# Turning the residual sum x2 (three of four column groups) and the input p by VectorE's 32x32 blocks out of DRAM instead of by TensorE

## The chip, the cores and the metric

The kernel runs on one core of a Trainium2 chip. Its time is the device time of one execution in microseconds (us); lower is better. The time before is the median of three runs, 1085.27 us (1084.38 to 1087.19).

## The reference

One decoder layer on 512 positions and 2048 channels, all in float32. Cut to what matters here:

```
h = rms_norm(x, norm_g);  z = h @ w_in                  # 2048 -> 6272 columns
y_rwkv = ...             # 16 heads x 64, delta-rule recurrence over 512 positions, gate
y_pool = ...             # 4 groups x 256, trailing means, small linear map, gate
y_mix  = concat(y_rwkv, y_pool)
x2  = x + y_mix @ w_out
gate = sigmoid(x2 @ w_pg + b_pg)
x3  = x2 + gate * (p @ w_ple)
out = rms_norm(x3, final_g)
```

A matrix product on TensorE contracts over the partition axis. `x2 @ w_pg` therefore needs x2 with its channels on the partitions, while the sum `x + y_mix @ w_out` comes out with positions on the partitions. The same holds for `p @ w_ple`. So x2 and p must be turned (transposed) before they can be multiplied.

## The kernel before, in words

Every large product is made of three matmuls in fp32r (`mm3`, L155 to L158): each operand is split into a rounded part `hi` and a rest `lo`, and hi·hi, hi·lo and lo·hi are added up in PSUM. A weight tile is loaded by a DMA that SyncE's queue issues (`raw`, L129), ScalarE makes `whi` by a cast (L132), VectorE makes `wlo` by a subtraction (L133). `raw`, `whi` and `wlo` have four buffers each, so the DMA of a tile waits until the subtraction of the tile four places earlier is done, and a cast waits until TensorE has used up the tile four places earlier.

The program has these stages:

1. RMSNorm of x, and x turned into `hhi`/`hlo`.
2. The head stage: eight pairs of heads, one after another (`recur`, `gather`, `prepare`, `scores`, `invert`). A pair's recurrence is a chain TensorE, VectorE, TensorE, ScalarE over eight chunks. TensorE never waits for it idly: between its steps `pump(n)` puts in n matmuls of a long stream (`stream`), which holds the z projections of later pairs, the pool group (`pool_unit`) and, in the last pair, the embedding product (`embed_unit`). In this stage TensorE keeps program order. The job `"p"` of the stream turns p: eight 128x128 transposes on TensorE into the PSUM tile `ppt`, each half then split into `phi` and `plo`. p itself comes by two DMAs that ScalarE's queue issues into `pn` (L927), which takes the buffer that `ar` of the last pair but one leaves.
3. The output projection: four column groups `ec` of 512 columns. Each has 16 steps (one weight tile of `w_out` per step, in the order of `order`), and each step has 12 matmuls: four position tiles times three. The sums stand in four of five PSUM accumulators that go round. At a group's end VectorE adds x to the four accumulators (L1026, tile `x2_{ec}_{tt}`; the trace calls it `x`), ScalarE's queue writes each sum to DRAM (`x2d`, L1027), and `turn` (L1029) turns it: 16 transposes on TensorE into PSUM (`px`, L1033), then four casts (L137) and four subtractions (L138) into `x2hi` and `x2lo`. For the first three groups `turn` runs right behind the group. For the last it runs as `aside`, inside the first group of the next stage.
4. The gate: the product with `w_pg` in four column groups, 16 steps each. The sum x2 is read back from `x2d` (`fetch`, L1133), and gate, embedding and final norm follow per position tile.

Instructions outside the head stage are placed by a scheduler with priorities; each engine then runs its own list in order, and so does each DMA queue.

Of the kernel before, what the change touches and what calls it, by code (L numbers as in the profile page):

```python
# [9 lines left out]
F32 = mybir.dt.float32  # L10
# [3 lines left out]
ALU = mybir.AluOpType  # L14

P = 128
T = 512
D = 2048
KT = D // P
NT = T // P  # L20
# [5 lines left out]
DPLE = 256  # L26
# [8 lines left out]
def trunk_kernel(ctx: ExitStack, tc: tile.TileContext, x, p, norm_g, w_in, mu, w0, w_up, a0, a_up,  # L35
                 k_k, k_a, r_k, ln_w, ln_b, w_pool, pool_scale, w_out, w_ple, w_pg, b_pg, final_g, out):
    nc = tc.nc
    PSUM = bass.MemoryType.PSUM
    x, p, w_in, w_out, w_ple, w_pg = x[0], p[0, 0], w_in[0], w_out[0], w_ple[0], w_pg[0]
    out = out[0]  # L40

    cst = ctx.enter_context(tc.tile_pool(name="cst", bufs=1))
    dram = ctx.enter_context(tc.tile_pool(name="dram", bufs=2, space=bass.MemoryType.DRAM))
# [4 lines left out]
    psM = s2.enter_context(tc.tile_pool(name="psM", bufs=3, space=PSUM))  # L48
# [24 lines left out]
    ident = cst.tile([P, P], F32, name="ident")  # L73
# [20 lines left out]
    for h in range(2):  # L94
        rows = slice(64 * h, 64 * h + 64)
# [30 lines left out]

    def wsplit(src, kt, n, nm):
        raw = wp.tile([P, kt, n], F32, name=f"raw_{nm}", tag="raw")
        nc.sync.dma_start(out=raw, in_=src)  # L129
        hi = wp.tile([P, kt, n], F32R, name=f"whi_{nm}", tag="whi")  # L130
        lo = wp.tile([P, kt, n], F32R, name=f"wlo_{nm}", tag="wlo")
        nc.scalar.copy(hi, raw)  # L132
        nc.vector.tensor_tensor(lo, raw, hi.bitcast(F32), ALU.subtract)  # L133
        return hi, lo

    def split(hi, lo, src):
        c_ = nc.scalar.copy(hi, src)  # L137
        nc.vector.tensor_tensor(lo, src, hi.bitcast(F32), ALU.subtract)  # L138
        return c_
# [20 lines left out]
    def tr(*a):  # L160
        i = nc.tensor.transpose(*a)
        return tc.keep_in_program_order(i) if pin[0] else i

    def mm3(ps, wh, wl, xh, xl, first, last):
        mm(ps, wh, xh, start=first, stop=False)
        mm(ps, wh, xl, start=False, stop=False)
        return mm(ps, wl, xh, start=False, stop=last)
# [26 lines left out]
    EC = 512  # L194
# [12 lines left out]
    for kind, nm, j in jobs:  # L207
# [7 lines left out]
        else:  # L215
            g, i = j // 4, j % 2
# [7 lines left out]
    order = [8, 9, 10, 11, 12, 13, 0, 1, 2, 3, 4, 5, 6, 7, 14, 15]  # L224
# [47 lines left out]
    pt = psM.tile([P, T], F32, name="pt_prm", tag="m")  # L272
# [188 lines left out]
    def stream():  # L461
        for kind, nm, j in jobs:
            if kind == "b":
                yield from pool_unit(j)
                continue
            if kind == "e":
                yield from embed_unit(j)
                continue
            if kind == "p":
                for k in range(2):  # L470
                    pt = psM.tile([P, T], F32, name=f"ppt{k}", tag="m")
                    for tt in range(NT):
                        tr(pt[:, tt * P:(tt + 1) * P], pn[0][:, tt, k * P:(k + 1) * P], ident)
                    a_ = rw.tile([P, T], F32R, name=f"phi{k}", tag=("sk", "sr")[k], bufs=2)
                    b_ = rw.tile([P, T], F32R, name=f"plo{k}", tag=("sv", "sg")[k], bufs=2)
                    split(a_, b_, pt)
                    phl.append((a_, b_))
                yield 3
                continue
            ps = psA.tile([P, T], F32, name=f"z{nm}{j}", tag="acc")  # L480
            yield from zcols(ps, f"{nm}{j}")
            t_ = rw.tile([P, T], F32, name=f"s{nm}{j}", tag=f"s{nm}", bufs=2)
            if nm == "g":
                silu2(ps, t_)
            else:
                shifted(ps, t_, {"r": 0, "k": 8, "v": 16}[nm] + j)
            zt[nm, j] = t_
# [429 lines left out]
    for j in range(NJ):  # L917
        def between():
            pump(H3 if j + 1 < NJ else HC[2])
            if j + 1 < NJ:  # L920
                scores(j + 1)
                pump_to(H2)

        if j + 1 == NJ:
            pn.append(rw.tile([P, NT, DPLE], F32, name="pn", tag="ar", bufs=2))
            for h in range(2):
                nc.scalar.dma_start(out=pn[0][:, 2 * h:2 * h + 2, :],  # L927
                                    in_=p[256 * h:256 * h + 256, :].rearrange("(t p) q -> p t q", p=P))
        if j + 1 < NJ:
            prepare(j + 1)  # L930
        elif gates:
            gates.pop()()
        recur(j, invert(j + 1) if j + 1 < NJ else iter(()), between)
        if j + 1 < NJ:
            gather(j + 1)
# [21 lines left out]

    x2hi = hp.tile([P, KT, T], F32R, name="x2hi", tag="ahi")
    x2lo = hp.tile([P, KT, T], F32R, name="x2lo", tag="alo")
    x2d = dram.tile([T, D], F32, name="x2d", bufs=1)  # L960

    KEEP, LATE = 8, 4
    TP = 40
# [4 lines left out]
        pool, tag = (psB, "accb") if nacc[0] % 5 in (1, 2, 3) else (psA, "acc")  # L968
        return pool.tile([P, EC], F32, name=nm, tag=tag)

    def proj(w, hi_, lo_, ec, nm, ks=range(KT), tts=range(NT), keep=None, aside=None):
        acc = {tt: acc_tile(f"acc_{nm}{ec}_{tt}") for tt in tts}
        for i, k in enumerate(ks):
            src = w[k * P:(k + 1) * P, ec * EC:(ec + 1) * EC].unsqueeze(1)
            if nm == "o" and ec == 0 and i + AHEAD < KT:
                load_y(ks[i + AHEAD])
            if (f"{nm}{ec}_{k}", 0) in ready:
                wh, wl = ready.pop((f"{nm}{ec}_{k}", 0))
            elif nm == "o" and ec == 0 and i < 4:
                wh, wl = chunk(f"{nm}{ec}_{k}", 0)  # L980
            elif keep is None or LATE <= i < KT - KEEP:
                wh, wl = wsplit(src, 1, EC, f"{nm}{ec}_{k}")
            else:
                raw = wp.tile([P, 1, EC], F32, name=f"raw_{nm}{ec}_{k}", tag="raw")
                nc.sync.dma_start(out=raw, in_=src)
                if i < 2:
                    if i == 0:
                        two = [pp.tile([P, 2, EC], F32R, name=f"{g}k", tag=g, bufs=1) for g in ("dh", "dl")]
                    wh, wl = (g[:, i:i + 1, :] for g in two)
                else:  # L990
                    own = i < KT - 4
                    wh, wl = ((kp_ if own else wp).tile([P, 1, EC], F32R, name=f"{g}k{k}",
                                                        tag=f"{g}k{k}" if own else g) for g in ("whi", "wlo"))
                split(wh, wl, raw)
                keep[k] = (wh, wl)
                if i >= LATE:
                    continue
            for tt in tts if keep is None or i >= LATE else tts[:-1]:
                ts_ = slice(tt * P, (tt + 1) * P)
                first = i == (LATE if keep is not None and tt == NT - 1 else 0)  # L1000
                e_ = mm3(acc[tt], hi_[:, k, ts_], lo_[:, k, ts_], wh[:, 0, :], wl[:, 0, :], first, i == KT - 1)
            if aside is not None and i == 2:
                with tc.issue_after(e_.ins):
                    hi = aside()
                with tc.issue_after(hi.ins):
                    recall(0, lp)
        return acc

    ples = {}

    def recall(ec, pool):
        ples[ec] = []
        for tt in range(NT):
            t_ = pool.tile([P, EC], F32, name=f"pler{ec}_{tt}", tag="ple", bufs=4)
            nc.scalar.dma_start(out=t_, in_=pled[tt * P:(tt + 1) * P, ec * EC:(ec + 1) * EC])
            ples[ec].append(t_)

    for ec in range(D // EC):
        es = slice(ec * EC, (ec + 1) * EC)
        acc = proj(w_out, yhi, ylo, ec, "o", order)  # L1020
        x2 = []
        for tt in range(NT):
            rows = slice(tt * P, (tt + 1) * P)
            t_ = pp.tile([P, EC], F32, name=f"x2_{ec}_{tt}", tag=("u", "sw")[tt // 2])
            nc.scalar.dma_start(out=t_, in_=x[rows, es])
            nc.vector.tensor_tensor(t_, acc[tt], t_, ALU.add)  # L1026
            nc.scalar.dma_start(out=x2d[rows, es], in_=t_)  # L1027
            x2.append(t_)
        def turn(ec=ec, x2=x2):  # L1029
            for i in range(EC // P):  # L1030
                pt = psM.tile([P, T], F32, name=f"px2_{ec}_{i}", tag="m")
                for tt in range(NT):
                    nc.tensor.transpose(pt[:, tt * P:(tt + 1) * P], x2[tt][:, i * P:(i + 1) * P], ident)  # L1033
                hi = split(x2hi[:, 4 * ec + i, :], x2lo[:, 4 * ec + i, :], pt)
            return hi


        if ec < D // EC - 1:
            turn()

    sy.close()

# [1 line left out]
    with tc.tile_pool(name="fp", bufs=2) as fp, tc.tile_pool(name="kp_", bufs=1) as kp_:  # L1044
# [86 lines left out]

        def fetch(ec, tt):
            x2_ = fp.tile([P, EC], F32, name=f"x2r{ec}_{tt}", tag="x2r", bufs=4)  # L1133
            nc.scalar.dma_start(out=x2_, in_=x2d[tt * P:(tt + 1) * P, ec * EC:(ec + 1) * EC])
            pre[tt] = (x2_, ple[tt])

        for ec in range(LAST):
# [74 lines left out]
```

## Time and profile before

| | |
|---|---|
| median of 3 runs | 1085.27 us (1084.38 to 1087.19) |
| the profiled execution | 1082.7 us, of which the span of its instructions is 1081.0 us |
| TensorE (PE) busy | 1056.6 us, 98% of the span |
| VectorE (DVE) busy | 714.0 us, 66% |
| ScalarE (ACT) busy | 441.5 us, 41% |
| DMA | 146.94 MB, mean 136 GB/s |

How to read the views. PE is TensorE's matmuls, PEld its weight loads, which run beside them; DVE is VectorE, ACT is ScalarE, SPq and ACTq are the DMA queues that SyncE and ScalarE feed. Times count from the start of the span. A matmul's own duration is modelled and overlaps the next one's, so what a matmul costs TensorE is read from the distance between starts, not from its mean duration. The chain of waits is followed back from the last instruction: each row is a stretch in which that work alone held up the end.

### The profile page before, as it was taken

How to read it: one execution, taken by the hardware profiler on the slowest of the kernel's cores; microseconds unless marked ns; L12 is line 12 of the kernel's file. 1: busy time of each engine (PE TensorE's matmuls, PEld its weight loads, DVE VectorE, ACT ScalarE, POOL GpSimd, SP SyncE). 2: the span in 40 equal slices, each digit the busy share in tenths (PEclk: the TensorE clock that was granted, in tenths of full speed). 3: DMA queues.
4: the chain of work that ended last, by engine and by line, in shares of the span. 5: the costliest groups of instructions: out<-in, count | busy, mean ns of one | idle time of the engine just before them, and what ended most of it. 6: DMA issues, size and time to landing. Idle time of an engine off the chain costs nothing.

```text
span 1081.0 us, 17106 instructions
## 1 busy us (share of the span) xinstructions
PE 1056.6 (98%) x5996; PEld 872.1 (81%) x5996; DVE 714.0 (66%) x1851; ACT 441.5 (41%) x901; POOL 75.0 (7%) x180
## 2 busy tenths in 40 slices
PE   5999999999999999999999999999999999999996
PEld 4888878888888887878788788888888888888885
DVE  6676978888779789787887857563432424445356
ACT  7633435335335354353352344553222222333337
POOL 2100010110110100200101201000000000000000
PEclk9999999999999999999999999999999999999999
DMA  7434443342634533434435343774434428355434
GB/s 236 117 115 111 139 116 88 116 120 74 168 88 114 144 89 105 120 89 112 106 91 158 100 129 111 239 243 141 171 121 143 166 98 271 122 182 161 169 98 156
DMA packets 212916, 146.94 MB, mean 136 GB/s; under 512 B 68085, under 2 KB 173150, under 8 KB 212830
## 3 DMA queue, kind: packets, MB, share of 16 engines
q1 hardware_dynamic: 192126, 112.28, 35.9%
q10 hardware_dynamic: 20704, 33.56, 9.4%
q8 instruction: 47, 0.77, 0.3%
q14 instruction: 39, 0.32, 0.1%
HBM read 122.21 MB, written 23.07 MB: 134 GB/s over the span
## 4 chain that ended last, share of the span: by engine, by line
PE 91%; DVE 4%; DMA 3%; ACT 2%; issue 1%; ACTq 0%; SPq 0%; DVEq 0%
PE acc_o L157 16%; PE acc_g L157 16%; PE zb L157 14%; PE zv L157 8%; PE zg L157 8%; PE zr L157 8%; PE zk L157 7%; PE py L157 2%; PE pu L157 2%; PE pple L157 2%; PE pm L157 1%; DMA n<-nd 1%; PE pp L157 1%; PE ps L157 1%; DMA xt<-in_x_dram 1%; PE pmv L157 1%
## 5 line engine op out<-in xcount | busy, mean ns | idle before, releaser
L133 DVE TENSOR_TENSOR wlo_g<-raw_g,whi_g 128x512 fp32r<-128x512 f32 x84 | 57.0, 685 | 74.4 <-ACT whi_g L132 72.3
L157 PE MATMUL zb<-hhi,whi_b 128*128 128x512 f32 x256 | 106.0, 414 | 0.0
L133 DVE TENSOR_TENSOR wlo_o<-raw_o,whi_o 128x512 fp32r<-128x512 f32 x64 | 43.9, 690 | 90.9 <-ACT whi_o L132 90.8
L157 PE MATMUL zb<-hhi,wlo_b 128*128 128x512 f32 x256 | 100.4, 392 | 0.0
L157 PE MATMUL acc_o<-whi_o,ylo 128*128 128x512 f32 x256 | 100.2, 391 | 0.0
L157 PE MATMUL acc_o<-whi_o,yhi 128*128 128x512 f32 x256 | 99.9, 390 | 0.0
L157 PE MATMUL zb<-hlo,whi_b 128*128 128x512 f32 x256 | 99.8, 390 | 0.0
L157 PE MATMUL acc_o<-wlo_o,yhi 128*128 128x512 f32 x256 | 99.7, 389 | 0.0
L132 ACT CAST whi_g<-raw_g 128x512 fp32r<-128x512 f32 x84 | 52.0, 621 | 105.3 <-PE acc_g L157 58.9
L157 PE MATMUL acc_g<-whi_g,x2hi 128*128 128x512 f32 x208 | 81.2, 391 | 0.0
L832 POOL TENSOR_SCALAR s0p<-sbd,pw 64x64 f32<-64x64 f32 x96 | 58.0, 604 | 332.0 <-DVE sbd L825 243.5
L157 PE MATMUL acc_g<-wlo_g,x2hi 128*128 128x512 f32 x208 | 80.9, 389 | 0.0
L157 PE MATMUL acc_g<-whi_g,x2lo 128*128 128x512 f32 x208 | 80.6, 389 | 0.0
L132 ACT CAST whi_o<-raw_o 128x512 fp32r<-128x512 f32 x64 | 39.9, 623 | 96.3 <-PE acc_o L157 96.3
L132 ACT CAST whi_b<-raw_b 128x512 fp32r<-128x512 f32 x64 | 39.7, 621 | 86.7 <-PE zb L157 29.2
L133 DVE TENSOR_TENSOR wlo_b<-raw_b,whi_b 128x512 fp32r<-128x512 f32 x64 | 43.6, 683 | 27.3 <-ACT whi_b L132 27.1
L157 PEld LDWEIGHTS zb<-hhi,wlo_b 128*128 128x128 f32 x256 | 48.0, 188 | 10.9
L678 DVE TENSOR_TENSOR xw<-xw,tm 128x60 f32<-128x60 f32 (+24 forms) x248 | 52.1, 210 | 7.0
L157 PEld LDWEIGHTS acc_o<-wlo_o,yhi 128*128 128x128 f32 x256 | 48.1, 188 | 9.9
L157 PEld LDWEIGHTS acc_o<-whi_o,ylo 128*128 128x128 f32 x256 | 48.1, 188 | 9.8
L157 PEld LDWEIGHTS acc_o<-whi_o,yhi 128*128 128x128 f32 x256 | 48.1, 188 | 9.7
L157 PEld LDWEIGHTS zb<-hhi,whi_b 128*128 128x128 f32 x256 | 48.2, 188 | 8.3
(283 smaller groups left out, 2529.6 us busy)
## 6 DMA issues: line engine op xcount, KB each, us to landing
raw_b<-in_w_in_dram SPq DMA_DIRECT2D x64, 256.0 KB
raw_o<-in_w_out_dram SPq DMA_DIRECT2D x64, 256.0 KB
raw_g<-in_w_pg_dram SPq DMA_DIRECT2D x64, 256.0 KB
raw_k<-in_w_in_dram SPq DMA_DIRECT2D x32, 256.0 KB
raw_r<-in_w_in_dram SPq DMA_DIRECT2D x32, 256.0 KB
raw_v<-in_w_in_dram SPq DMA_DIRECT2D x32, 256.0 KB
raw_g<-in_w_in_dram SPq DMA_DIRECT2D x32, 256.0 KB
bkd<-bk SPq DMA_DIRECT2D x8, 512.0 KB
```

The lines of the kernel that those rows point to most:

```text
L132: nc.scalar.copy(hi, raw)
L133: nc.vector.tensor_tensor(lo, raw, hi.bitcast(F32), ALU.subtract)
L157: i = nc.tensor.matmul(*a, **k)
L678: nc.vector.tensor_tensor(xw[:, 0:n_, s + 1:32], xw[:, 0:n_, s + 1:32], tm[:, 0:n_, 0:w_], ALU.add)
L832: nc.gpsimd.tensor_scalar(s0p[hc, :], nxt[hc, hc], pcn[hc], None, ALU.mult)
```

## The change

- **x2, groups 0 to 2.** `x2d` is laid out anew, as (column group, 128-column chunk, position, 128 columns). The 16 transposes on TensorE of each of these groups are gone. Instead the blocks are read back from `x2d` by 16 DMAs on SyncE's queue into `x2g`: a DMA brings 32 columns of a chunk, for all 512 positions, as 512 pieces of 128 bytes, so that block (b, q) lies where VectorE's transpose of 32x32 blocks turns it into place. VectorE then turns a chunk with one instruction of 128x512 (`STREAM_TRANSPOSE`, into `x2t`), and the split into `x2hi`/`x2lo` follows as before, out of SBUF instead of PSUM. This hangs in the next group's steps (`side`): reads from step 5 on, three DMAs a step, and turns at steps 8, 9, 11 and 12, each placed behind that step's weight DMA, cast and subtraction.
- **x2, group 3** is turned by TensorE as before. Its place (`aside`) moves by one step: it now stands before the third step's products, not behind them.
- **p** is read in the same blocked way by eight DMAs of 64 KB on SyncE's queue (two of 256 KB on ScalarE's before), and turned by two VectorE instructions instead of eight transposes on TensorE.
- **x2d** is now written, and read by `fetch`, in pieces of 512 bytes instead of 2048.

```diff
-                for k in range(2):
-                    pt = psM.tile([P, T], F32, name=f"ppt{k}", tag="m")
-                    for tt in range(NT):
-                        tr(pt[:, tt * P:(tt + 1) * P], pn[0][:, tt, k * P:(k + 1) * P], ident)
+                    pt = rw.tile([P, T], F32, name=f"ppt{k}", tag=("kk", "kp")[k])
+                    nc.vector.transpose(pt.rearrange("p (b k) -> p b k", k=32), pn[0][:, k])
...
-            for h in range(2):
-                nc.scalar.dma_start(out=pn[0][:, 2 * h:2 * h + 2, :],
-                                    in_=p[256 * h:256 * h + 256, :].rearrange("(t p) q -> p t q", p=P))
+            for q in range(4):
+                for c in range(2):
+                    nc.sync.dma_start(out=pn[0][32 * q:32 * q + 32, c],
+                                      in_=p[:, c * P + 32 * q:c * P + 32 * q + 32].rearrange("(b k) i -> k b i", k=32))
...
-    x2d = dram.tile([T, D], F32, name="x2d", bufs=1)
+    x2d = dram.tile([D // EC, EC // P, T, P], F32, name="x2d", bufs=1)
...
-            for tt in tts if keep is None or i >= LATE else tts[:-1]:
-                ...
             if aside is not None and i == 2:
...
+            if side is not None:
+                side(i)
+            for tt in tts if keep is None or i >= LATE else tts[:-1]:
+                ...
...
+    RD0, RDN, TURNS = 5, 3, (8, 9, 11, 12)
...
-        acc = proj(w_out, yhi, ylo, ec, "o", order)
+        acc = proj(w_out, yhi, ylo, ec, "o", order, side=side)
...
-            nc.scalar.dma_start(out=x2d[rows, es], in_=t_)
+            nc.scalar.dma_start(out=x2d[ec, :, rows, :].rearrange("c t e -> t c e"),
+                                in_=t_.rearrange("p (c e) -> p c e", e=P))
...
+        def turner(blocks, turned, ec=ec):
+            parts = [(c, q) for c in range(EC // P) for q in range(4)]
+
+            def side(i):
+                with tc.issue_after(wmade[0].ins), tc.issue_after(wmade[1].ins), tc.issue_after(wmade[2].ins):
+                    if i >= RD0:
+                        for c, q in parts[:RDN]:
+                            nc.sync.dma_start(out=blocks[32 * q:32 * q + 32, c],
+                                              in_=x2d[ec, c].rearrange("(b k) (q i) -> q k b i", k=32, i=32)[q])
+                        del parts[:RDN]
+                    if i in TURNS:
+                        c = TURNS.index(i)
+                        t_ = turned(c)
+                        nc.vector.transpose(t_.rearrange("p (b k) -> p b k", k=32), blocks[:, c])
+                        split(x2hi[:, 4 * ec + c, :], x2lo[:, 4 * ec + c, :], t_)
...
-            turn()
+            side = turner(ymp.tile([P, EC // P, T // 32, 32], F32, name=f"x2g{ec}", tag="x2g"),
+                          lambda i: ymp.tile([P, T], F32, name="x2t", tag="x2t"))
```

What the scheduler made of it is seen in two places. The first is SyncE's list in the second group of the output projection, in the changed kernel; `raw_o1_k` is the weight tile of row block k, and since the order of the steps is 8, 9, ..., 13, 0, 1, 2, ..., the tile `raw_o1_2` belongs to step 8.

```order
L129 DMA raw_o1_0_8542<-in_w_out_dram 128x512
L129 DMA raw_o1_1_8563<-in_w_out_dram 128x512
L1045 DMA x2g0_8426<-x2d_8101 32x16x32 x9
L129 DMA raw_o1_2_8584<-in_w_out_dram 128x512
L1045 DMA x2g0_8426<-x2d_8101 32x16x32 x3
L129 DMA raw_o1_3_8609<-in_w_out_dram 128x512
L1045 DMA x2g0_8426<-x2d_8101 32x16x32 x3
L129 DMA raw_o1_4_8634<-in_w_out_dram 128x512
L1045 DMA x2g0_8426<-x2d_8101 32x16x32
L129 DMA raw_o1_5_8653<-in_w_out_dram 128x512
```

Before, the weight tiles stand alone there. Now nine of the block reads stand between the tiles of steps 7 and 8, three between 8 and 9, three between 9 and 10, and one between 10 and 11.

The second place is VectorE's list at `gather` of the last pair. `y17` is the turned diagonal block of that pair's inverse (it is read from `x17`, which a DMA brings), for which TensorE's next product of the chain (`pq`) waits; `wlo_b12_k` is a weight tile of the stream, `ysb6` the scaling of the pair before. First the kernel before:

```order
L732 STREAM_TRANSPOSE y17_7360<-x17_7214 32x256
L133 TENSOR_TENSOR wlo_b12_0_4333<-raw_b12_0_4330,whi_b12_0_4332 128x512
L732 STREAM_TRANSPOSE y17_7360<-x17_7214 32x256
L873 TENSOR_SCALAR ysb6_6780<-ysb6_6780,mvr6_7284,rs86_7301 128x64 x6
L133 TENSOR_TENSOR wlo_b12_1_4355<-raw_b12_1_4352,whi_b12_1_4354 128x512
```

And the changed kernel:

```order
L133 TENSOR_TENSOR wlo_b12_0_4333<-raw_b12_0_4330,whi_b12_0_4332 128x512
L734 STREAM_TRANSPOSE y17_7360<-x17_7214 32x256
L133 TENSOR_TENSOR wlo_b12_1_4355<-raw_b12_1_4352,whi_b12_1_4354 128x512
L734 STREAM_TRANSPOSE y17_7360<-x17_7214 32x256
L875 TENSOR_SCALAR ysb6_6780<-ysb6_6780,mvr6_7284,rs86_7301 128x64 x8
```

Each half of `y17` now stands one weight subtraction later. On SyncE's list the reads of p now stand among the DMAs that carry the inverse. On TensorE's list nothing moves but this: the 8 + 48 transposes are gone, the transposes of group 3 stand 12 matmuls earlier, and in steps 8 to 11 of the groups the matmuls that need `whi` alone are drawn ahead of those that need `wlo`.

More of the change, by code (lines that the diff above doesn't have):

```diff
@@ L128, in wsplit @@
         raw = wp.tile([P, kt, n], F32, name=f"raw_{nm}", tag="raw")
-        nc.sync.dma_start(out=raw, in_=src)
+        made = [nc.sync.dma_start(out=raw, in_=src)]
         hi = wp.tile([P, kt, n], F32R, name=f"whi_{nm}", tag="whi")
         lo = wp.tile([P, kt, n], F32R, name=f"wlo_{nm}", tag="wlo")
-        nc.scalar.copy(hi, raw)
-        nc.vector.tensor_tensor(lo, raw, hi.bitcast(F32), ALU.subtract)
+        made.append(nc.scalar.copy(hi, raw))
+        made.append(nc.vector.tensor_tensor(lo, raw, hi.bitcast(F32), ALU.subtract))
+        wmade[:] = made
         return hi, lo
+    wmade = []
     def split(hi, lo, src):
@@ L924, in trunk_kernel @@
         if j + 1 == NJ:
-            pn.append(rw.tile([P, NT, DPLE], F32, name="pn", tag="ar", bufs=2))
-            for h in range(2):
-                nc.scalar.dma_start(out=pn[0][:, 2 * h:2 * h + 2, :],
-                                    in_=p[256 * h:256 * h + 256, :].rearrange("(t p) q -> p t q", p=P))
+            pn.append(rw.tile([P, 2, T // 32, 32], F32, name="pn", tag="ar", bufs=2))
+            for q in range(4):
+                for c in range(2):
+                    nc.sync.dma_start(out=pn[0][32 * q:32 * q + 32, c],
+                                      in_=p[:, c * P + 32 * q:c * P + 32 * q + 32].rearrange("(b k) i -> k b i", k=32))
         if j + 1 < NJ:
@@ L969, in acc_tile, with proj @@
         return pool.tile([P, EC], F32, name=nm, tag=tag)
-    def proj(w, hi_, lo_, ec, nm, ks=range(KT), tts=range(NT), keep=None, aside=None):
+    def proj(w, hi_, lo_, ec, nm, ks=range(KT), tts=range(NT), keep=None, side=None, aside=None):
         acc = {tt: acc_tile(f"acc_{nm}{ec}_{tt}") for tt in tts}
@@ L997, in proj @@
                     continue
-            for tt in tts if keep is None or i >= LATE else tts[:-1]:
-                ts_ = slice(tt * P, (tt + 1) * P)
-                first = i == (LATE if keep is not None and tt == NT - 1 else 0)
-                e_ = mm3(acc[tt], hi_[:, k, ts_], lo_[:, k, ts_], wh[:, 0, :], wl[:, 0, :], first, i == KT - 1)
             if aside is not None and i == 2:
@@ L1006, in proj @@
                     recall(0, lp)
-        return acc
+            if side is not None:
+                side(i)
+            for tt in tts if keep is None or i >= LATE else tts[:-1]:
+                ts_ = slice(tt * P, (tt + 1) * P)
+                first = i == (LATE if keep is not None and tt == NT - 1 else 0)
+                e_ = mm3(acc[tt], hi_[:, k, ts_], lo_[:, k, ts_], wh[:, 0, :], wl[:, 0, :], first, i == KT - 1)
+        return acc
+    RD0, RDN, TURNS = 5, 3, (8, 9, 11, 12)
+    side = None
     ples = {}
@@ L1026, in trunk_kernel @@
             nc.vector.tensor_tensor(t_, acc[tt], t_, ALU.add)
-            nc.scalar.dma_start(out=x2d[rows, es], in_=t_)
+            nc.scalar.dma_start(out=x2d[ec, :, rows, :].rearrange("c t e -> t c e"),
+                                in_=t_.rearrange("p (c e) -> p c e", e=P))
             x2.append(t_)
+        def turner(blocks, turned, ec=ec):
[12 more added lines that the diff above has]
+                        split(x2hi[:, 4 * ec + c, :], x2lo[:, 4 * ec + c, :], t_)
+            return side
         def turn(ec=ec, x2=x2):
@@ L1133, in fetch @@
             x2_ = fp.tile([P, EC], F32, name=f"x2r{ec}_{tt}", tag="x2r", bufs=4)
-            nc.scalar.dma_start(out=x2_, in_=x2d[tt * P:(tt + 1) * P, ec * EC:(ec + 1) * EC])
+            nc.scalar.dma_start(out=x2_.rearrange("p (c e) -> p c e", e=P),
+                                in_=x2d[ec, :, tt * P:(tt + 1) * P, :].rearrange("c t e -> t c e"))
             pre[tt] = (x2_, ple[tt])
```

## The prediction

> **What bounds the kernel now.** I read the page first, for the engine that sets the end.
>
> ```profile
> span 1081.0 us, 17106 instructions
> PE 1056.6 (98%) x5996; PEld 872.1 (81%) x5996; DVE 714.0 (66%) x1851; ACT 441.5 (41%) x901; POOL 75.0 (7%) x180
> PE 91%; DVE 4%; DMA 3%; ACT 2%; issue 1%; ACTq 0%; SPq 0%; DVEq 0%
> ```
>
> TensorE is busy for 98% of the span and carries 91% of the chain that ended last. That alone is a mean over stages, so next I took the stages that the change touches, in the chain in order of time. The columns are start, length and what; x192 is the number of matmuls in a stretch.
>
> ```profile
> 715.63 43.52 PE acc_o L157 x192
> 763.54 41.06 PE acc_o L157 x181
> 808.98 41.07 PE acc_o L157 x181
> 854.42 41.06 PE acc_o L157 x181
> 895.49 8.17 PE acc_g L157 x36
> ```
>
> These are the four groups of the output projection and the start of the gate. The first group has no turn in it: 192 matmuls without a break in 43.52 us, 0.2267 us each, so a step of 12 takes 2.72 us and the group ends at 715.63 + 43.52 = 759.15. The other three have the turn of the group before at their head. They end at 763.54 + 41.06 = 804.60, then at 850.05 and 895.48: 45.45, 45.45 and 45.43 us. TensorE is the chain all through; nothing else interrupts it.
>
> For p, the same view in the last pair of heads:
>
> ```profile
> 649.56 1.39 PE zb L157 x6
> 650.95 0.87 PE ppt L161 x8
> 651.82 0.22 PE py L157 x2
> 652.04 1.39 PE zb L157 x6
> ```
>
> Here too the transposes stand in the chain between work that fills TensorE.
>
> **The change part by part.** *The turns of groups 0 to 2 leave TensorE.* Each costs the difference of a group with and without it: 45.45 − 43.52 = 1.93, again 1.93, and 1.91: together 5.77 us, 0.12 us per transpose. *The eight transposes of p* cost 0.87 us by their row. So TensorE's part of the chain becomes 6.64 us shorter, provided that nothing is late in place of it.
>
> The price is not the duration that the transposes have in the table of groups:
>
> ```profile
> L1033 PE MATMUL px<-ident,x 128*128 128x128 f32 x64 | 9.1, 277 | 0.0
> L161 PE MATMUL ppt<-ident,pn 128*128 128x128 f32 x8 | 1.0, 272 | 0.0
> ```
>
> 277 ns is the mean of one that overlaps its neighbours; 64 of them keep TensorE busy for 9.1 us, not 17.7. The Trainium skill's page "TensorE: Matmul & The Clock Gate", section on PE-mode transpose, gives about 275 ns for one 128x128 transpose inside a kernel; by that figure 56 fewer would be worth 15.4 us, an estimate, and the trace agrees with the figure as a duration but not as the cost of one in a row of transposes.
>
> *What VectorE and ScalarE get.* VectorE gets 12 + 2 turns of 128x512; a turn of this shape is in the trace for the keys:
>
> ```profile
> L617 DVE STREAM_TRANSPOSE bkn<-bg 128x512 f32<-128x512 f32 x16 | 10.9, 697 | 0.0
> 759.10:804.60 45.50, 45.50 (x211) 37.65 (x210) 15.92 (x25) 11.92 (x20) 0.00 (x0) 1.00 0.40 139
> ```
>
> The second row is the second group's window: after the span come busy times of PE, PEld, DVE, ACT and POOL, the clock, the DMA share and GB/s. Four turns add 4 x 0.70 = 2.8 us to VectorE's 15.92 of 45.50; the casts and subtractions only move within the group. A step then holds at most one weight subtraction, one turn and one x2 subtraction, some 2.1 of its 2.72 us. I cost this at nothing; what hides it is VectorE's idle 29 us per group. Group 2's turned sum is first needed eight steps into the gate, well behind its last turn, so no deadline replaces TensorE's.
>
> *What DMA gets.* Per group 16 reads of 512 pieces of 128 bytes, and the same for p in eight reads. Two stretches of the trace show pieces of both sizes on one queue, the first mostly reads of 128 bytes, the second a weight load in pieces of 512:
>
> ```profile
> DMA packets 1044, 0.15 MB, mean 154 GB/s; under 512 B 983, under 2 KB 1044, under 8 KB 1044
> q1 hardware_dynamic: 1044, 0.15, 90.4%
> DMA packets 272, 0.13 MB, mean 131 GB/s; under 512 B 16, under 2 KB 272, under 8 KB 272
> q1 hardware_dynamic: 272, 0.13, 44.5%
> ```
>
> Each stretch is 1 us of 16 engines: 0.904 x 16 / 1044 = 13.9 ns for a short piece, 0.445 x 16 / 272 = 26.2 ns for one of 512 bytes. A group's 8192 short pieces thus take 8192 x 13.9 / 16 = 7.1 us of all engines, while they are 40% busy over 45.5 us. The Trainium skill's page "DMA: Bandwidth & Descriptors", section Specifications, speaks against such reads: full rate needs transfers of at least 512 bytes, and smaller ones are read, modified and written. The trace agrees in that a byte costs about twice as much, yet a short piece takes half the time of a long one; were each as dear as a long one, a group would need 13.4 us, which the idle 60% still holds.
>
> *The order on SyncE's queue* is the part that can hurt: SyncE issues in order, so the weight tile of step 8 waits behind nine block reads, and these wait until the sums stand in DRAM. The rows for it are SyncE's issues of the keys' block reads, which are twice as large (least, median and longest in ns), one of them, VectorE's additions and ScalarE's writes at the second group's head, the transfers there, and a weight tile's cast and subtraction:
>
> ```profile
> L662 SPq DMA_DIRECT2D bg<-bkd x32: 568/617/3007, 85.0 to 593.5; - x32
> 218.58 2.76 SPq L662 DMA_DIRECT2D bg<-bkd  x1
> 757.74 2.48 DVE L1026 TENSOR_TENSOR x<-acc_o,x 128x512 f32<-128x512 f32 x4
> 758.46 2.12 ACTq L1027 DMA_DIRECT2D x2d<-x  x4
> q10 hardware_dynamic: 576, 1.05, 68.9%
> 772.04 0.62 ACT L132 CAST whi_o<-raw_o 128x512 fp32r<-128x512 f32 x1 [2.09 <-PE acc_o L157]
> L133 DVE TENSOR_TENSOR wlo_o<-raw_o,whi_o 128x512 fp32r<-128x512 f32 x64 | 43.9, 690 | 90.9 <-ACT whi_o L132 90.8
> ```
>
> The writes are issued by 760.58. The row for q10 covers 759.5 to 763.5: 1.05 MB, 0.689 x 4 x 16 / 576 = 77 ns per packet, 2.8 us in all. In 512-byte pieces it is 2048 x 26.2 / 16 = 3.4 us. So I put the landing at about 764.2. Nine reads at the median issue, 0.6 us each, end at 769.6, and the tile of step 8 follows. A read issued at 628.28 (below) lets its reader start at 630.63, so 2.35 us later; the tile is there at about 772.3. Its cast could not start before step 4 is done with its buffer, 759.15 + 5 x 2.72 = 772.75 (the row at 772.04 is such a cast, waiting for TensorE), and step 8 begins at 759.15 + 8 x 2.72 = 780.9. Cast and subtraction take 1.31 us: some 6 us are left. Cost: nothing.
>
> *The last pair.* There the reads of p stand among the DMAs of the inverse, and both halves of `y17` stand one weight subtraction later on VectorE:
>
> ```profile
> 628.28 0.45 SPq L689 DMA_DIRECT2D x<-xd  x1
> 630.63 0.43 DVE L732 STREAM_TRANSPOSE y<-x 32x256 f32<-32x256 f32 x1 [0.53 <-DMA x<-xd]
> 632.31 0.67 DVE L133 TENSOR_TENSOR wlo_b<-raw_b,whi_b 128x512 fp32r<-128x512 f32 x1
> 633.64 0.69 PE L157 MATMUL pq<-y,mt 32*32 32x32 f32 x32
> ```
>
> The second half ended at 631.06 and `pq` starts at 633.64. Now it stands behind the subtraction that ends at 632.98, so it ends at 633.41, 0.2 us before TensorE comes to it. I take 0.1 us of wait; the bounds are 0 and 1.4, one more subtraction and one more turn in front (0.67 + 0.70). The two turns of p fall between steps of the last recurrence; 1.39 us of filler (the row at 652.04) lies between `py` and the next step of the chain, and a turn of 0.70 takes half of it. Nothing for that.
>
> *The 512-byte pieces of x2d* make a transfer of 256 KB some 0.2 us longer; its readers in the gate stand behind whole groups of 16 steps. *Group 3's turn* keeps its 16 transposes; 12 matmuls earlier it stands at 895.49 + 24 x 0.2267 = 900.9, over 3 us behind the sums. Both nothing.
>
> The sum: 1082.7 (the profiled execution; 1081.0 of it the span, 1.7 around it) − 5.77 − 0.87 + 0.1 = 1076.2 us. The profiled execution was 2.6 us faster than the median of the runs shown, 1085.27, so for a median I add 2.6 again: **1078.8 us**, 0.6% faster. About 0.3%, 3.2 us, is what a measurement of this kernel can tell from no change.
>
> **The rivals.** *SyncE's queue stalls* (slower). The trace has no nine short reads in a row, and the row at 218.58 shows one issue that took 2.76 us, behind other transfers that had filled the queue. From 764.2 the nine may take until 780.9 − 1.31 − 2.35 − 0.33 = 776.9 before step 8 waits: 12.7 us, 1.41 us each. Above that TensorE idles in three groups; at (12.7 + 2.2) / 9 = 1.66 us each the 6.6 us are used up. At 2.76 us each the nine take 24.8, step 8 waits 12.1 us, and the three groups cost 36.4: 1078.8 + 36.4 = 1115 us. Against it: the median of the 32 block reads is 0.62 us although each is twice as large, and nothing else stands in SyncE's queue there but weight tiles. Chance 0.06.
>
> *The waits come back* (no change). The transposes may have covered the change of accumulators: if TensorE waits 1.93 us at each group's head instead, only p's 0.77 is left, 1084.5 us. For it speaks that there are five accumulators for four in use. Against it: the four additions take 0.62 us each, so the first ends at 758.36 and the fourth at 760.22, and the second tile of the next group's first step, which takes the first one's place, comes at 759.15 + 0.68 = 759.83. Each place is free about 1.4 us early. Chance 0.08.
>
> *The transposes are worth their recorded duration* (faster): 48 x 0.277 + 8 x 0.272 = 15.5 us, 1069.8 us. The group lengths speak against it. Chance 0.02.
>
> *The change does not do what it says:* the turns could still stand on TensorE. The order shows that they are gone, so I give that nothing.
>
> **How the numbers follow.** My forecast has 0.80, the three rivals 0.06, 0.08 and 0.02; 0.04 is left for what I don't see, half of it a gain above 3.2 us, half a loss. The forecast's own range: the wait of the last pair (0 to 1.4), up to 0.5 us per group for a late step, and the runs, which spread from 0.9 below to 1.9 above their median: 1077 to 1081.5. For 8 in 10 with what rivals would move a part of the way I widen it to 1076 to 1083. Faster by over 0.3%: 0.80 + 0.02 + 0.02 = 0.84, of which I move 0.01 to no change for the spread of the runs: 0.83. No change: 0.08 + 0.01 = 0.09. Slower: 0.06 + 0.02 = 0.08.
>
> **What would show it.** In the profile after, the second to fourth groups of the output projection take 43.5 us from end to end instead of 45.45, without idle time before `acc_o`; `px` has 16 transposes instead of 64; the tile of step 8 is issued near 769.6 − 1 (everything from p on comes 0.9 us earlier); `y` of the last pair ends just before `pq`. The prediction is wrong if SyncE's block reads take over 1.4 us each, if TensorE waits for `whi_o` or `wlo_o` at step 8, if it waits at a group's head for an addition, or if the head stage before p has become longer.

## The result and the profile after

| | before | after |
|---|---|---|
| median | 1084.97 us (6 runs, 1084.38 to 1087.19) | 1079.47 us (6 runs, 1078.01 to 1081.80) |
| ratio | | 0.9947, 95% interval 0.9933 to 0.9961 |
| the profiled execution | 1082.7 us, span 1081.0 | 1079.2 us, span 1077.5 |

The change takes 5.5 us off, 0.5%. The forecast was 1078.8 us. The page of after first: its span, the engines, and the chain by engine.

```profile
span 1077.5 us, 17094 instructions
PE 1050.0 (97%) x5940; PEld 865.9 (80%) x5940; DVE 722.8 (67%) x1865; ACT 442.2 (41%) x901; POOL 75.0 (7%) x180
PE 89%; DVE 5%; DMA 3%; ACT 2%; issue 1%; SPq 0%; ACTq 0%; DVEq 0%
```

TensorE has 56 matmuls fewer (5940 against 5996) and is 6.6 us less busy. Then the chain in order of time, at the output projection and the gate of after.

```profile
717.79 174.08 PE acc_o L160 x768
891.87 5.44 PE acc_g L160 x24
900.22 166.31 PE acc_g L160 x739
```

What were four stretches with a turn between them is one stretch of 768 matmuls without a break, 174.08 us, 0.2267 each. Before, the same work went from 715.63 to 895.49, 179.86 us. That is 5.78 us less; the working said 5.77. From the gate's start to the end of its last row the length is the same, 1066.53 − 891.87 = 174.66, against 174.65 before (895.49 to 1070.14). So neither the moved turn of group 3 nor the 512-byte pieces of `x2d` cost anything there.

At p the chain of after has no transposes between the filler of the stream (`zb`) and `py` any more:

```profile
652.61 1.39 PE zb L160 x6
654.00 0.22 PE py L160 x2
```

So both gains of the working are in the trace, 5.78 and 0.87 us, 6.65 together. Yet the span is only 3.5 us shorter. The missing 3 us lie ahead of p: the `py` near 590 us comes 3.04 us later than in the profile of before, in a stretch in which both programs hold the same instructions. The waits of TensorE and VectorE name the place: TensorE does wait for the recurrence now and then. First the kernel before, then the one after; the columns are the total in us, how often, and the longest.

```profile
PE py L157 <- DVE sbd L825: 1.4, 2, 0.9
DVE tm L674 <- DMA n<-nd: 18.4, 8, 5.1
```

```profile
PE py L160 <- DVE sbd L827: 3.9, 5, 1.3
DVE tm L676 <- DMA n<-nd: 21.9, 8, 5.4
```

`tm` is the first instruction of a pair's inversion on VectorE; it waits for a read of 256 KB of `nd` from DRAM (`n`), and `sbd`, a step of the recurrence, stands behind it in VectorE's order. TensorE waits for `sbd`. These reads came later in total in the profile after. Whether the change did that or an execution differs by so much from the next is what the first experiments ask.

Then SyncE's queue in the second group, the risk of the forecast: issues of after, start and length.

```profile
766.47 7.65 SPq L1045 DMA_DIRECT2D x2g<-x2d  x9
774.21 0.43 SPq L129 DMA_DIRECT2D raw_o<-in_w_out_dram  x1
...
778.20 0.62 ACT L132 CAST whi_o<-raw_o 128x512 fp32r<-128x512 f32 x1 [5.34 <-DMA raw_o<-in_w_out_dram]
778.85 0.69 DVE L133 TENSOR_TENSOR wlo_o<-raw_o,whi_o 128x512 fp32r<-128x512 f32 x1 [5.27 <-ACT whi_o L132]
```

The nine reads take from 766.47 to 774.21, 0.86 us each; the tile of step 8 is issued there, cast at 778.20 and split by 779.54. Step 8 begins at 717.79 + 43.52 + 8 x 2.72 = 783.07. TensorE does not wait, and 3.5 us are left. Before, only weight tiles stood in this queue. The reads do not run in idle DMA time: the window of the nine in after shows the DMA engines 95% busy (last columns: clock, DMA share, GB/s), and the same stretch of the kernel before, 764.31 to 772.05, is 73% busy already, without them.

```profile
766.47:774.21 7.74, 7.74 (x36) 6.42 (x35) 2.08 (x3) 1.87 (x3) 0.00 (x0) 1.00 0.95 202
```

And the last pair in after, where the second half of `y17` now stands behind a weight subtraction:

```profile
635.23 0.69 DVE L133 TENSOR_TENSOR wlo_b<-raw_b,whi_b 128x512 fp32r<-128x512 f32 x1 [1.01 <-ACT whi_b L132]
635.84 0.42 DVE L734 STREAM_TRANSPOSE y<-x 32x256 f32<-32x256 f32 x1
636.69 0.69 PE L160 MATMUL pq<-y,mt 32*32 32x32 f32 x32
```

It ends at 636.26, 0.4 us before `pq`; there is no wait.

### The profile page after: what moved, and what is told of

It is laid out like the page before. It is cut to its first block, busy times and chain, and to the rows that moved or that the text cites. A ratio compares the mean times of both kernels' runs of the same rounds, so it can differ in the third digit from the quotient of the medians.

```text
span 1077.5 us, 17094 instructions
## 1 busy us (share of the span) xinstructions
PE 1050.0 (97%) x5940; PEld 865.9 (80%) x5940; DVE 722.8 (67%) x1865; ACT 442.2 (41%) x901; POOL 75.0 (7%) x180
## 4 chain that ended last, share of the span: by engine, by line
PE 89%; DVE 5%; DMA 3%; ACT 2%; issue 1%; SPq 0%; ACTq 0%; DVEq 0%
PE acc_o L160 16%; PE acc_g L160 16%; PE zb L160 15%; PE zv L160 8%; PE zr L160 8%; PE zg L160 6%; PE zk L160 6%; DMA n<-nd 2%; PE py L160 2%; PE pple L160 2%; PE pu L160 2%; PE pm L160 1%; PE pp L160 1%; PE ps L160 1%; PE pmv L160 1%
## 5 line engine op out<-in xcount | busy, mean ns | idle before, releaser
L160 PE MATMUL acc_o<-whi_o,yhi 128*128 128x512 f32 x256 | 94.7, 389 | 0.0
L676 DVE TENSOR_TENSOR tm<-xw,n 128x60 f32<-128x60 f32 (+10 forms) x240 | 50.7, 211 | 6.4
```

Source lines behind the costliest of these rows:

```text
L160: i = nc.tensor.matmul(*a, **k)
L676: nc.vector.tensor_tensor(tm[:, 0:n_, 0:w_], xin[:, 0:n_, s:s + 1].to_broadcast([P, n_, w_]), nb[s // 16][:, s % 16:s % 16 + 1, s + 1:32]. ...
```

## The experiments

### Two second profiles, and each part alone

The kernel before and the changed kernel were profiled again without any edit, and the two parts of the change were made apart. x2 alone is the changed kernel with p taken back:

```diff
-                    pt = rw.tile([P, T], F32, name=f"ppt{k}", tag=("kk", "kp")[k])
-                    nc.vector.transpose(pt.rearrange("p (b k) -> p b k", k=32), pn[0][:, k])
+                    pt = psM.tile([P, T], F32, name=f"ppt{k}", tag="m")
+                    for tt in range(NT):
+                        tr(pt[:, tt * P:(tt + 1) * P], pn[0][:, tt, k * P:(k + 1) * P], ident)
```

(and ScalarE's two loads of p). p alone is the kernel before with the same lines the other way round and the eight block reads of p.

> The kernel before, unchanged, for a second profile. In the profile after, the head stage loses 3.04 us before 600 us, in a stretch in which both programs hold the same instructions. Theory A (the head stage differs by some 3 us from one execution to the next): the first matmul of the output projection stands anywhere from 714 to 719 us, not at 715.63 again, and TensorE's waits at `py` for `sbd` add up to something between 1 and 5 us. Theory B (the change itself lengthens the head stage): it starts at 715.6 to within 0.3 us, with waits at `py` of 1.4 us, as in the first profile. Either way the groups take 43.52, 45.45, 45.45 and 45.43 us.

> The changed kernel, unchanged, for a second profile. Theory A: the start of the output projection moves against the first profile's 717.79 us by up to some 3 us either way, its four groups again take 174.1 us without a break, and from there to the end nothing moves. Theory B: it starts at 717.8 to within 0.3 us, with waits at `py` of about 4 us, in the same places.

> Only the x2 part: p is read by ScalarE and turned by eight transposes on TensorE as before. The prediction's terms: 3 x 1.93 = 5.8 us faster than before, ratio 0.9947, the four groups and the gate as in the changed kernel (768 matmuls in one unbroken stretch of 174.1 us). Rival (the 5.3 us that the change brought come partly from p, or the x2 part is hurt by its own short reads): a gain of under 4 us, with waits at `whi_o` or `wlo_o` in steps 8 to 11. If the x2 part were what lengthened the head stage, the first product of the output projection would again start 3 us late here.

> Only the p part: p by eight blocked reads on SyncE's queue and two turns on VectorE, x2 as before. Theory A, the prediction's terms: 0.9 us faster less a wait of at most 0.1 at `pq`, ratio 0.9993, so no difference that can be told from none. Theory B (p's eight reads on SyncE's queue lengthen the head stage by the 3 us that the profile after lost there): slower by about 2 us, ratio 1.002, and the first product of the output projection starts at 717.8 us or later.

**The second profile of before** took 1085.61 us. Its chain at the output projection, and its waits:

```profile
718.56 43.52 PE acc_o L157 x192
```

```profile
PE py L157 <- DVE sbd L825: 3.6, 4, 1.3
DVE tm L674 <- DMA n<-nd: 21.7, 8, 4.7
```

The same program begins the projection 2.93 us later than in its first profile, with the waits that the profile after had; 2.2 of the 2.93 us are TensorE's longer waits at `py`. One pair, in the first profile of before and then in the second:

```profile
586.82 0.19 DVE L674 TENSOR_TENSOR tm<-i,n 128x31 f32<-128x31 f32 x1 [2.66 <-DMA n<-nd]
590.34 0.49 PE L157 MATMUL py<-sbd,ar 128*128 128x128 f32 x2 [0.52 <-DVE sbd L825]
```

```profile
589.77 0.19 DVE L674 TENSOR_TENSOR tm<-i,n 128x31 f32<-128x31 f32 x1 [3.10 <-DMA n<-nd]
593.29 0.49 PE L157 MATMUL py<-sbd,ar 128*128 128x128 f32 x2 [0.96 <-DVE sbd L825]
```

VectorE waits 0.44 us longer for the read, TensorE 0.44 us longer for `sbd`, in the same instruction of the same kernel. The pair's reads were issued at 580.10 and at 582.61, so `tm` starts 6.72 us behind the issue in the one and 7.16 in the other. That is theory A: these reads do not land equally fast from one execution to the next, and the head stage passes it on. Why they land later is not shown. The second profile of after took 1078.35 us and began the projection at 716.94 instead of 717.79; theory B asked for the same place to within 0.3. The first profile of before, at 1082.7 us, was one of the shortest executions of that kernel: in the three later sets its runs went from 1082.62 to 1089.61.

**x2 alone**: 1079.44 us against 1086.14 beside it, ratio 0.9942 (0.9925 to 0.9959). In us 6.3, between 4.5 and 8.1, with 5.8 expected. Its chain has the same unbroken stretch:

```profile
718.05 174.08 PE acc_o L160 x768
```

**p alone**: 1084.31 us, ratio 0.9980 (0.9968 to 0.9992), a gain of 0.9 to 3.5 us. Theory B, a loss of 2 us, is out. The expected 0.87 lies at the near end of the interval. In its chain `py` follows the six `zb` directly, at 654.30; what is gone is seen in the second profile of before. First p alone, then that profile:

```profile
652.91 1.39 PE zb L157 x6
```

```profile
653.88 0.87 PE ppt L161 x8
```

Theory B's other sign did appear: the projection of p alone starts at 718.09, behind 717.8. But the kernel before starts it at 718.56 in its second profile, so that sign tells nothing. Over all profiles of this document, the four with p on TensorE start the projection between 715.63 and 718.56 (mean 717.4), the ten with p on VectorE between 716.69 and 719.32 (mean 717.8). The scatter is larger than 0.87 us: these starts show neither p's gain nor a loss of that size, and for p's gain at the end of the program only the times speak.

### The price of a transpose

In the kernel before, each transpose of groups 0 to 2 is issued twice into the same place:

```diff
                     nc.tensor.transpose(pt[:, tt * P:(tt + 1) * P], x2[tt][:, i * P:(i + 1) * P], ident)
+                    if ec < D // EC - 1:
+                        nc.tensor.transpose(pt[:, tt * P:(tt + 1) * P], x2[tt][:, i * P:(i + 1) * P], ident)
```

> The kernel before, with every transpose of groups 0 to 2 issued twice into the same place of PSUM: 48 transposes more, the output the same. Theory (the price of a transpose in a row is the distance between starts, 0.12 us): the second to fourth groups take 45.45 + 1.93 = 47.4 us each, 5.8 us more in all, ratio 1.0053. Rival (the recorded duration, 277 ns): 49.9 us each, 13.3 us more in all, ratio 1.0122. Second rival (the transposes filled a wait for the accumulators, which the change then found empty for another reason): less than 1 us a group.

1090.06 us, ratio 1.0044 (1.0029 to 1.0060), 3.1 to 6.5 us. The windows of its second and third groups, from end to end:

```profile
760.71:807.84 47.13, 47.13 (x226) 39.43 (x225) 15.95 (x25) 12.12 (x20) 0.00 (x0) 1.00 0.40 134
807.84:854.99 47.15, 47.15 (x227) 39.42 (x225) 15.95 (x25) 12.12 (x20) 0.00 (x0) 1.00 0.41 134
```

45.45 has become 47.13 and 47.15: 1.70 us for 16 more, 0.106 each. The recorded duration, 277 ns, would have made it 49.9, and a cover of waits under 46.5; both are out. The first 16 cost 1.93, 0.23 us more than the second 16. A part of it is seen in the traces: at the second group's head the transposes stand in three runs, in two when they are doubled, and the first product behind each run starts 0.31 to 0.32 us ahead of the next instead of 0.227. At p eight transposes in one run cost 0.87 us, 0.109 each, and no more.

### SyncE's queue

Twice the reads (the second ones into `x2s`, a place in DRAM that nothing reads), and the same reads in halves, both in the changed kernel:

```diff
-                            nc.sync.dma_start(out=blocks[32 * q:32 * q + 32, c],
-                                              in_=x2d[ec, c].rearrange("(b k) (q i) -> q k b i", k=32, i=32)[q])
+                            for to in (blocks[32 * q:32 * q + 32, c], x2s[ec, c, q]):
+                                nc.sync.dma_start(out=to,
+                                                  in_=x2d[ec, c].rearrange("(b k) (q i) -> q k b i", k=32, i=32)[q])
```

```diff
+                            for h in range(2):
+                                nc.sync.dma_start(out=blocks[32 * q:32 * q + 32, c, 8 * h:8 * h + 8],
+                                                  in_=x2d[ec, c].rearrange("(b k) (q i) -> q k b i", k=32, i=32)[q][:, 8 * h:8 * h + 8])
```

> The changed kernel, with each of the 16 block reads of a group followed by an equal one into DRAM that nobody reads: 18 reads instead of nine between the weight tiles of steps 7 and 8, then 6, 6 and 2. In the profile after, the nine took 0.86 us each and the tile of step 8 stood 3.5 us ahead of its need. Theory (SyncE's queue sets the margin): 18 x 0.86 = 15.5 us, 7.7 more, so TensorE waits some 4 us at step 8 in each of three groups and again 2 to 3 us at steps 9 and 10: 12 to 30 us slower than the changed kernel, with `whi_o` and `wlo_o` in TensorE's waits. Rival (the reads were bound by the landing of the sums or by something else that passes, not by their number): no wait of TensorE, no change against the changed kernel's 1079 us.

> The changed kernel, with each block read split into two of 256 pieces: the same bytes and pieces in 32 issues, 12 of them ahead of the tile of step 7 and 18 ahead of that of step 8. Theory (what the queue takes goes by pieces): 18 x 0.43 = 7.7 us as before, the tile of step 8 is issued at about the same time, no wait, no change of time against the changed kernel. Rival (it goes by issues, 0.86 us each): the tile of step 7 is issued 12 x 0.86 = 10.3 us behind the first read and comes some 2 us late, that of step 8 some 4 us late: over 12 us slower.

**Twice**: 1096.34 us, ratio 1.0103 (1.0079 to 1.0126), some 17 us slower than the changed kernel was in its first runs. SyncE's issues in the second group, and the waits of TensorE:

```profile
767.71 0.33 SPq L1047 DMA_DIRECT2D x2g<-x2d  x1
...
781.35 0.56 SPq L129 DMA_DIRECT2D raw_o<-in_w_out_dram  x1
```

```profile
PE acc_o L160 <- ACT whi_o L132: 8.0, 7, 1.7
...
PE acc_o L160 <- DVE wlo_o L133: 1.8, 8, 0.2
```

18 reads take 13.6 us, 0.76 each, and the tile of step 8 is late, so the queue does set the margin. The waits are shorter than expected (0.7 to 1.7 us at a time, not 4), but each brings a second loss. The whole projection, first in the changed kernel and then here:

```profile
717.79:891.87 174.08, 174.08 (x770) 144.19 (x769) 75.80 (x117) 52.73 (x88) 0.00 (x0) 1.00 0.63 171
```

```profile
719.04:909.28 190.24, 180.38 (x769) 144.65 (x769) 75.14 (x116) 52.71 (x88) 0.00 (x0) 0.99 0.66 172
786.50:791.00 4.50, 4.50 (x13) 3.53 (x14) 2.44 (x4) 1.24 (x2) 0.00 (x0) 0.62 0.78 153
```

16.2 us more. By the table TensorE stands idle for 9.9 of them and is busy 6.3 longer with the same matmuls; but a matmul's modelled duration, 0.39 us and more, is longer than the 0.227 it costs, so the distances between starts say better where the time went. 9.4 us lie ahead of the first matmul of eight late tiles. 4.0 lie between that matmul and the next, which needs the tile's subtraction, 0.69 us of VectorE behind the cast: the two stand 0.72 to 0.73 us apart. 1.6 lie in eight matmuls that stand 0.427 us apart, behind one of the waits; the last row is that stretch, with its granted clock of 0.62. The other 1.2 lie in the matmuls right behind the late ones.

**Halves**: 1082.22 us, ratio 0.9976 (0.9962 to 0.9990), 3 to 4 us slower than the changed kernel was in the other sets. The theory that it goes by pieces fell. The issues:

```profile
763.89 9.03 SPq L1046 DMA_DIRECT2D x2g<-x2d  x12
773.01 0.40 SPq L129 DMA_DIRECT2D raw_o<-in_w_out_dram  x1
773.45 4.22 SPq L1046 DMA_DIRECT2D x2g<-x2d  x6
777.78 0.40 SPq L129 DMA_DIRECT2D raw_o<-in_w_out_dram  x1
```

```profile
716.69:894.41 177.72, 175.58 (x770) 143.76 (x769) 75.32 (x116) 53.48 (x88) 0.00 (x0) 1.00 0.60 166
```

A read of 256 pieces takes 0.72 to 0.76 us of the queue on average, far from half of what one of 512 takes (0.86 in the changed kernel, 0.76 with twice the reads). The averages hold gaps in which nothing is issued; the median of the issues alone is 0.45 us for the 96 reads of 256 pieces and 0.49 for the 48 of 512 in the changed kernel. TensorE idles 2.1 us over the projection and is busy 1.5 us longer. The price goes by issues far more than by pieces; the rival had the cause, and its size (over 12 us) was too large.

### Who issues the reads

The changed kernel was timed again, and then with the block reads of x2 issued by GpSimd (`nc.gpsimd.dma_start` for `nc.sync.dma_start`, nothing else).

> The changed kernel, unchanged, beside the three below on one chip, so that they can be set against it: ratio to before 0.9947 as in the first runs, the unbroken stretch of 768 matmuls again 174.1 us.

> The changed kernel, with the 48 block reads of x2 issued by GpSimd instead of SyncE. Theory (in the changed kernel SyncE's queue costs no time, since its tile of step 8 stands 3.5 us ahead): no change of time against the changed kernel, and the tile of step 8 issued some 8 us earlier, at the time of the kernel before. Rival (the reads themselves, by their pieces, slow the weight tiles on the DMA engines, or GpSimd issues them so slowly that the turns come late): TensorE waits at `whi_o` or `x2hi`, a microsecond or more per group.

The changed kernel: 1078.31 us, ratio 0.9935 (0.9921 to 0.9950), with its stretch of 174.08 us again. With GpSimd's queue: 1079.00 us, ratio 0.9940 (0.9925 to 0.9954). SyncE's queue of the latter, and its chain:

```profile
757.23 27.57 SPq L129 DMA_DIRECT2D raw_o<-in_w_out_dram  x11
```

```profile
717.74 174.08 PE acc_o L160 x768
```

Only weight tiles are left in SyncE's queue, the tile of step 8 is issued at 765.43 instead of 774.21, and nothing gets faster: the same unbroken stretch. In the changed kernel the nine reads cost margin, not time.

### The fourth group

Group 3 is turned by VectorE too, in the first group of the gate. `turn` and its 16 transposes go; each chunk has its own buffer for the blocks, from those of `u` and `sw`, and the first gate group gets `side`.

```diff
-                    hi = aside()
-                with tc.issue_after(hi.ins):
+                with tc.issue_after(e_.ins):
                     recall(0, lp)
...
+            side = turner([pp.tile([P, T // 32, 32], F32, name=f"x2g{ec}_{c}", tag=("u", "sw")[c // 2])
+                           for c in range(EC // P)], lambda i: pp.tile([P, T], F32, name="x2t", tag="sgp", bufs=1))
```

> The changed kernel, with group 3 turned by VectorE too, in the first group of the gate, so that no transposes of x2 are left on TensorE. Theory: its last 16 transposes are worth another 16 x 0.12 = 1.9 us, since the turned chunks of group 3 are needed only in steps 12 to 15 of the gate: ratio to before 0.993, some 7.4 us faster. Rival (the reads come after the sums of group 3 and share SyncE's queue with the gate's tiles, of which 9 are first steps' due; steps 8 or 12 wait): no gain against the changed kernel, ratio 0.995, or worse.

1085.78 us, ratio 1.0009 (0.9997 to 1.0020): the whole gain of the change is lost again. Its issues on SyncE at the head of the gate, its wait, and two windows:

```profile
896.56 10.98 SPq L1043 DMA_DIRECT2D x2g<-x2d  x6
908.31 0.35 SPq L129 DMA_DIRECT2D raw_g<-in_w_pg_dram  x1
```

```profile
PE acc_g L160 <- ACT whi_g L132: 5.7, 1, 5.7
```

```profile
896.56:908.22 11.66, 11.66 (x53) 9.67 (x52) 1.59 (x3) 1.17 (x2) 0.00 (x0) 1.00 1.05 200
915.00:919.00 4.00, 3.27 (x7) 2.34 (x8) 1.34 (x3) 1.24 (x2) 0.00 (x0) 0.50 0.92 197
```

The weight tile behind six reads can be issued 11.66 us after the first of them, 1.94 us per read, in a stretch in which the DMA engines are full, most of it with the gate's operands. The chain says what the queue does in that time: it waits for two transfers to land, a block read and one of ScalarE's reads of x2.

```profile
896.56 7.38 DMA x2g<-x2d
903.96 4.24 DMA x2r<-x2d
```

The tile comes 5.7 us late, and the matmuls that follow run at a granted clock of 0.50. This is the first rival of the prediction, at a place that the change leaves alone, and with its price above the 1.41 us from which it was to decide.

Two ways out were tried: the reads of group 3 later, and with GpSimd as well.

```diff
-    RD0, RDN, TURNS = 5, 3, (8, 9, 11, 12)
+    PLAN = ((5, 3, (8, 9, 11, 12)),) * 3 + ((9, 4, (11, 12, 13, 14)),)
...
+            RD0, RDN, TURNS = PLAN[ec]
```

> All four groups turned by VectorE, with the reads of group 3 hung in steps 9 to 12 of the gate instead of 5 to 10, so that they stand behind the weight tile of step 9 on SyncE's queue and not ahead of that of step 7, and its turns in steps 11 to 14. In the first such kernel six reads took 11.7 us in a stretch in which the DMA engines were full, and the tile of step 7 came 5.7 us late. Theory (place, not number): by then the burst of gate operands is over and the reads take under 1 us each, no wait, 1.9 us faster than the changed kernel. Rival (the reads only move the stall to steps 10 to 12): waits of `whi_g` there, no gain or a loss.

> The same, with all block reads on GpSimd's queue, so that no weight tile stands behind one. Theory: no wait of TensorE, 1.9 us faster than the changed kernel, ratio to before 0.993. Rival (the DMA engines, not the queue, are what is full at the head of the gate): the reads of group 3 start as soon as the sums stand in DRAM, share the engines with the gate operands, and the weight tiles land late all the same: a wait of `whi_g` of several us around step 7.

**Later**: 1077.11 us (1074.38 to 1079.71), ratio 0.9919 (0.9902 to 0.9937). The chain has no break from the projection to the end of the gate:

```profile
719.32 174.08 PE acc_o L160 x768
893.40 173.33 PE acc_g L160 x768
```

The gate takes 173.33 us instead of 174.66: 1.3 us less, where 1.9 were expected. At its 51st matmul the kernel is 1.8 us ahead of the changed one, so the turn is worth what was said; 0.5 us go again further on, in distances of 0.33 to 0.46 us between starts near 931, 943 and 985, whose cause is not shown. Against the changed kernel beside it (1078.31, 1077.45 to 1079.42) the times alone do not separate the two, since the runs overlap; the gate in the traces does. The profile of this kernel has 5.9 us of waits at `py` in the head stage, which hides the gain in its span of 1077.7.

**With GpSimd's queue**: 1078.04 us, ratio 0.9939 (0.9921 to 0.9957). SyncE's weight tiles pass the reads now, and one comes late all the same:

```profile
898.54 12.68 DMA raw_g<-in_w_pg_dram
911.21 0.02 issue
911.23 3.57 ACTq L1084
```

```profile
PE acc_g L160 <- ACT whi_g L132: 2.2, 1, 2.2
```

A tile issued at 898.54 takes 12.68 us to land, and the cast behind it waits 3.57 us more, since ScalarE is held up in issuing a DMA of its own (`bB`, the bias). At this place the rival holds in part: the tile lands late though no read stands ahead of it in its queue. But the wait is 2.2 us and not several, and without ScalarE's 3.57 us it would not have come. The Trainium skill's page "DMA: Bandwidth & Descriptors", section "Issuing engines are not separate DMA queues", says that DMAs of all issuing engines run on the same 16 DMA engines, and that another issuer saves only the time of issuing; both runs with GpSimd agree.

## Why the prediction was right, step by step

- **x2 off TensorE, 5.77 us.** Shown: 5.78 in the profile, 6.3 (4.5 to 8.1) with this part alone, and the doubled transposes cost 1.70 us per 16. The choice of the distance between starts, and not the recorded duration, carried the forecast; the rival with 277 ns is out.
- **p, 0.87 us.** Shown in the chain at p; by time alone 0.9 to 3.5 us. The starts of the projection scatter too much to show it. The 0.1 us of wait at `pq` did not come: there is none.
- **VectorE's turns hidden.** The turns took 704 ns each (697 in the row used), and TensorE has no wait for `x2hi` or `x2lo` in the projection or the gate.
- **DMA hidden.** Right in its result. The reason was an average: 40% busy over a whole group. At the place where the reads run the engines were 73% busy before and are 95% busy now, which the average doesn't show.
- **SyncE's queue, "some 6 us left".** Right in its result, mis-sized: 3.5 us. Nine reads took 0.86 us each and not 0.6: seven were issued in 0.30 to 0.49 us, two took 1.4 and 1.6, and in two gaps of 0.9 and 0.5 us nothing was issued. The tile was cast 4.0 us behind its issue and not 2.35; the row taken for that was a read of 32 KB, and the tile has 256 KB. The sums landed where the step had put them: 764.2 + 2.2 for the later start is 766.4, and the first read is issued at 766.47. The stall that the rival described was real: it came with 18 reads, with 32 smaller ones, and at the gate.
- **The waits come back at the heads of groups.** They did not; there is no break there.
- **From the profile to the median.** Adding 2.6 us was needed: the first profile of before was a short one, by some 3 us in the head stage, as its second profile shows. Read profile against profile, the change would seem to bring 3.5 us. One of the working's own signs of being wrong, a longer head stage before p, did appear in the first profile of after, and the second profile of before shows that it appears without the change too.

## What to carry to other kernels

A transpose in a row on TensorE costs the distance between starts, and a group with and without it gives that number; the duration in a table of groups is more than twice as long. Work that goes to another engine through DRAM is paid in a queue: count the issues that are put ahead of a needed load, multiply by their price in that very stretch (0.49 us as the median issue of the 48 reads of the changed kernel, 0.86 on average with the gaps at 95% DMA, 1.94 at the head of the gate, most of it waiting for other transfers to land), and keep them out of stretches that are full. Before two profiles are subtracted, compare a stretch in which both programs are identical.

## What the runs showed of the hardware that was not expected

- **A late tile costs more than the wait for its cast.** With the reads doubled, eight late tiles brought 9.4 us ahead of their first matmul and 4.0 us more until the subtraction was there too. The clock comes on top, but seldom. Behind a wait of 5.7 us the granted clock was 0.50 for the 4 us of the window shown. Behind one of 1.3 us matmuls stood 0.427 us apart for 3.4 us (clock 0.62 over the 4.5 us shown), and behind the one of 2.2 us in the last kernel as well; behind the other late tiles of these kernels, with waits of up to 1.7 us, they were soon 0.227 us apart again. The Trainium skill's page "TensorE: Matmul & The Clock Gate", Part 1, gives about 3.4 us of idle time as the window after which the clock is halved; the 5.7 us agree, the 1.3 and 2.2 us do not. What decides it behind a shorter wait is not shown.
- **A read's issue costs about the same with 256 pieces as with 512**: 0.45 us against 0.49 as the median, 0.72 to 0.76 on average with the gaps against 0.76 to 0.86.
- **Going back from transposes to products costs something too**: the first product behind each run of transposes costs 0.08 to 0.09 us more than the others, so a turn in three runs is dearer than its 16 transposes.
- **Equal programs differ by 3 us in one stage**, and most of it is seen in waits for reads of 256 KB from DRAM, which land later in one execution than in the other, with VectorE's fixed order behind them.
